# Three weight sums of a projection unit: made by GpSimd in the raw tiles, at product P6

## The chip, the cores and the metric

The kernel runs on one core of a Trainium2 chip. The metric is the device time of one execution in microseconds (us); of several timed runs the median stands. A core has five engines that run their own queues of instructions: TensorE (PE; its weight loads are listed apart, as PEld), VectorE (DVE), ScalarE (ACT), GpSimd (POOL) and SyncE (SP, which here only issues transfers). They wait for one another through semaphores.

## The reference

One layer of a hybrid trunk over 2048 positions of width 1024, all in 32-bit floating point. Cut to what matters here:

```
xn = rmsnorm(x, norm1_g)
z  = xn @ w_in                      # 1024 x 4608, this is the projection of the change
u_pool, zq, zf, zi, zo, zg = split(z)
gates  = sigmoid(zg + b_gate)
ya = pool_mixer(u_pool) @ w_pa
yb = hgrn2_mixer(zq, zf, zi, zo) @ w_pb      # gated linear recurrence, in chunks
x  = x + (gates[0] * ya + gates[1] * yb) @ w_o
x  = x + conv_glu_ffn(rmsnorm(x, norm2_g))
return rmsnorm(x, final_g)
```

## The kernel before, in words

**Products.** A product of two 32-bit matrices is made from three PE products of a reduced format (`fp32r`): each 128x512 weight tile is split into a high part, which ACT makes with a cast (L231, `ops`), and a low part, which DVE makes by subtracting the high part from the original (L232). PE multiplies both with a split activation (`mm`, L148 in the trace).

**Units.** The projection `z = xn @ w_in` is cut into fourteen *units* (the table `PROJ`: kinds `fq`, `g` and `u`). A unit is two 128-column blocks of outputs; its weights are four *quarters* q0, q1, q2, q3 of 128x512. A scheme of Strassen's kind makes the 2x2 block product with seven products instead of eight. Four of them need a sum of quarters as their weight: P6 takes s2 = q0+q2+q3, P5 takes s1 = q2+q3, P7 takes s3 = q0+q2, and P3 takes s4 = s2+q1; P1, P2 and P4 take q0, q1 and q3 as they are. The order of a unit's products is P1, P6, P5, P7, P2, P4, P3 (`ORDER`). Their results stand in three PSUM banks: X (P1, P2), Z (P6, P7, P4) and V (P5, P3). After P1 ACT copies bank X to `e1`; after P6 DVE makes `u2` = e1 - Z (L1196, `u` in the trace), and after P7 it makes `u3` from Z (L1200); P7 and P4 can only overwrite bank Z when that is done. The names in the trace are `fr`, `gr` and `ur` for units of kinds `fq`, `g` and `u`.

**Two passes.** The sequence is worked in two halves. In the first pass (from about 97 to 500 us) the quarters are loaded by SP (L197) into *raw* tiles, and the four sums of each unit are made by POOL, one add each (L444, function `comb`). Each sum is also stored to DRAM by SP (L341, `kw...`), and in the second pass (from about 1357 us) the sums are simply loaded from there.

**Buffers.** Raw tiles turn in a ring of eight (`N_RAW`), converted weights in one of six (`N_OPS`), and everything else that is 128x512 (sums, gates, intermediate results of the recurrence) takes one of 77 *slots* (`N_SLOTS`), in the order in which they are asked for. A tile is free for its next owner when all that read it, stores included, has ended.

**What sets the order.** The program is written as a stream of conversions that runs up to four weight tiles ahead of PE (`LOOKAHEAD`): `convert` calls the product's function `fn`, which may issue adds, and then the cast and the subtraction; `load_ahead` issues raw loads as soon as the ring has a tile whose last reader has been converted; `store_kept` issues the stores of the sums that `keep` has listed. Besides the units run tasks, stepped every six matmuls, for the heads of the recurrence: on PE `pl` (L1026, attention), `po` (L1125 and L1127), `pt` (L1144); on DVE `f` (L1096), `ss` (L1117), `ot` (L1138); on ACT `oh` (L1146), the gates `gt` (L1446); on POOL the copies `qm` (L1011), the products `q` (L1409) and the roots `ro` (L690); on SP the loads of `v` and `z` (L968) and of `mx` (L961). A scheduler then puts the instructions of each engine in the order in which its own estimate lets them run, so an edit in one place can change the order of an engine elsewhere. After the units come the products `pa` and `pb`, in which DVE makes `ya` (L1519) from the gates `gl` (L961).

Of the kernel before, what the change touches and what calls it, by code (L numbers as in the profile page):

```python
# [81 lines left out]
def tile_trunk(  # L82
# [26 lines left out]
    def slot(name, cols=TB, dt=F32):  # L109
        return slots.tile([P, cols], dt, tag="s", name=name, padded_shape=[P, 528])  # L110
# [221 lines left out]
    def keep(key, t, later=False):  # L332

        nm = "kw" + "".join(str(c) for c in np.ravel(key[1])) + f"{key[0]}{key[2]}"
        kept[key] = dram.tile([P, 512], F32, tag=nm, name=nm)
        keeping.append((kept[key], t, later))
# [12 lines left out]
    SUM_OF = {"P5": "s1", "P6": "s2", "P7": "s3", "P3": "s4"}  # L349
# [42 lines left out]
    def plan_unit(key, src, kind, i, order, b0):  # L392
        mv, mg = proj_tiles(kind, i)
        if b0:
            unit = sums_of_unit(src, mv, mg, lambda p: lambda: kept["in", (kind, i), SUM_OF[p]])
        else:
            unit = weights_of_unit(src[mv], src[mg], (kind, i))
        for p in order:
            fn, raws = unit[p]()
            stream.op(key, fn, raws)  # L400
# [19 lines left out]
    def quarters(src_v, src_g):  # L420
        return [s[:, c * 512 : (c + 1) * 512] for s in (src_v, src_g) for c in range(2)]
# [10 lines left out]

    def weights_of_unit(src_v, src_g, unit):
        src = quarters(src_v, src_g)
        raws, tmp = {}, {}

        def raw(i):
            if i not in raws:
                raws[i] = stream.raw(src[i])
            return raws[i]  # L440

        def comb(nm, key, x0, x1):
            t = slot(f"{nm}{key}")
            pool.tensor_tensor(t, x0, x1, ALU.add)  # L444
            tmp[key] = t
            keep(("in", unit, key), t)
            return t

        def plan(p):
            if p == "P5":  # L450
                return (lambda nm: tmp["s1"]), []
            rs = [raw(i) for i in {"P1": (0,), "P2": (1,), "P4": (3,), "P6": (0, 2, 3),
                                   "P7": (0, 2), "P3": (1,)}[p]]

            def fn(nm):
                t = [r.tile for r in rs]
                if p == "P6":
                    comb(nm, "s1", t[1], t[2])
                    return comb(nm, "s2", tmp["s1"], t[0])
                if p == "P7":  # L460
                    return comb(nm, "s3", t[1], t[0])
                if p == "P3":
                    return comb(nm, "s4", tmp["s2"], t[0])
                return t[0]

            return fn, rs

        return {p: (lambda p=p: plan(p)) for p in ORDER}

    def up_order():  # L470
# [1407 lines left out]
```

## Time and profile before

| | |
|---|---|
| median of 3 timed runs | 2531.32 us (2531.08 to 2533.26) |
| the profiled execution | 2530.39 us, its span 2528.7 us |
| PE busy | 2507.8 us, 99% of the span |
| weight loads of PE | 2053.8 us, 81% |
| DVE busy | 1963.1 us, 78% |
| ACT busy | 1195.1 us, 47% |
| POOL busy | 746.3 us, 30% |
| granted clock of PE | 0.999 |

The span runs from the first to the last instruction in the trace; the execution's own time is 1.7 us longer. All times within the trace are counted from the start of the span. In lists of instructions stand the start, the duration, the engine, the line, the operation, and in brackets how long the engine had been idle before and what ended that. In a list of waits stand the waiting instruction, what released it, the sum of the waits, their number and the longest. In a chain of work each row is released by the one above it. A table of stretches gives each stretch's bounds and length, then the busy time and the number of instructions of PE, PEld, DVE, ACT and POOL, the granted clock, the share of the transfer engines and their GB/s.

### The profile page before, as it was taken

The numbers are of one execution on the slowest core, as the hardware profiler recorded it, in microseconds if no ns is written. First come the engines' busy times: TensorE is split into PE (matmuls) and PEld (weight loads), VectorE is DVE, ScalarE is ACT, GpSimd is POOL, SyncE is SP. The second block draws the span as 40 slices with busy tenths as digits, with TensorE's granted clock in tenths as the row PEclk, the third lists the DMA queues.
The fourth block names the chain that finished last, engine by engine and source line by source line (L and its number), as shares of the span: only waits on it lengthen the run. The fifth ranks groups of instructions, "written<-read, shape, count | busy, mean of one in ns | idle before, by whom it ended". The sixth has DMA issues, their size and how long they took to land.

```text
span 2528.7 us, 35641 instructions
## 1 busy us (share of the span) xinstructions
PE 2507.8 (99%) x11508; PEld 2053.8 (81%) x11508; DVE 1963.1 (78%) x3476; ACT 1195.1 (47%) x2250; POOL 746.3 (30%) x1127
## 2 busy tenths in 40 slices
PE   9999999999999999999999999999999999999998
PEld 7888888788888888888888888888888888888887
DVE  7788878598898777885596778665979988778755
ACT  6534443334555454554554444542355554445534
POOL 4333453003354334451320202200033432325410
PEclk9999999999999999999999999999999999999999
DMA  8877777777898879997344343447443454447852
GB/s 272 271 184 231 203 203 231 221 230 244 200 259 231 229 230 240 265 364 244 123 150 150 109 134 109 138 148 233 140 155 118 151 153 135 153 133 245 321 166 97
DMA packets 252331, 493.75 MB, mean 195 GB/s; under 512 B 26544, under 2 KB 43056, under 8 KB 251824
## 3 DMA queue, kind: packets, MB, share of 16 engines
q1 hardware_dynamic: 184512, 313.60, 39.2%
q0 software_dynamic: 42656, 112.74, 17.5%
q10 hardware_dynamic: 24976, 65.13, 7.5%
q8 instruction: 91, 1.49, 0.2%
q14 instruction: 96, 0.79, 0.1%
HBM read 381.79 MB, written 187.17 MB: 225 GB/s over the span
## 4 chain that ended last, share of the span: by engine, by line
PE 92%; DVE 3%; DMA 1%; ACT 1%; issue 1%; POOL 0%; SPq 0%; ACTq 0%; DVEq 0%; POOLq 0%
PE dn_P L148 16%; PE up_Z L148 15%; PE up_V L148 10%; PE up_X L148 10%; PE wo_P L148 6%; PE gr_Z L148 4%; PE pb L148 4%; PE pa L148 3%; PE gr_X L148 3%; PE io_Z L148 3%; PE gr_V L148 3%; PE fr_Z L148 2%; PE io_V L148 2%; PE fr_X L148 2%; PE fr_V L148 1%; PE pl L1026 1%
## 5 line engine op out<-in xcount | busy, mean ns | idle before, releaser
L231 ACT CAST ops<-raw 128x512 fp32r<-128x512 f32 x744 | 459.6, 621 | 816.0 <-PE dn_P L148 179.5
L232 DVE TENSOR_TENSOR ops<-raw,ops 128x512 fp32r<-128x512 f32 x744 | 555.3, 750 | 216.7 <-ACT ops L231 209.8
L1614 DVE SCALAR_TENSOR_TENSOR e<-h,cols,e 128x512 f32<-128x512 f32 x176 | 143.3, 819 | 31.0 <-ACT e L1612 25.4
L1612 ACT ACTIVATE e<-h,cols 128x512 f32<-128x512 f32 x176 | 142.2, 814 | 25.1 <-DVE h L1159 18.3
L1617 DVE SCALAR_TENSOR_TENSOR e<-h,cols,e 128x512 f32<-128x512 f32 x176 | 133.9, 770 | 2.5
L961 POOL DMA_DIRECT2D g_P<-dg_P x154 | 84.0, 547 | 159.8 <-PE dn_P L148 111.3
L1269 POOL TENSOR_TENSOR gf_P<-e,e 128x512 f32<-128x512 f32 x44 | 61.2, 1392 | 149.4 <-DVE e L1623 95.9
L1269 POOL TENSOR_TENSOR gf_P<-gf_P,e 128x512 f32<-128x512 f32 x44 | 59.3, 1347 | 71.9 <-DVE e L1623 71.5
L1409 POOL TENSOR_TENSOR q<-q,qs 128x512 f32<-128x512 f32 x16 | 21.6, 1347 | 187.5 <-ACT qs L1408 180.3
L1607 POOL COPY h<-h 128x2 f32<-128x2 f32 x88 | 39.9, 466 | 117.7 <-DVE h L1158 113.6
L1621 ACT ACTIVATE e<-e 128x512 f32<-128x512 f32 x88 | 55.6, 632 | 38.3 <-DVE e L1617 38.0
L1446 ACT ACTIVATE gt<-gt,cols 128x512 f32<-128x512 f32 x48 | 34.8, 725 | 79.5 <-DVE gt L1159 47.1
L1609 POOL COPY hist<-h 128x2 f32<-128x2 f32 x88 | 35.5, 404 | 117.9 <-DVE h L1159 116.1
L1159 DVE TENSOR_TENSOR h<-up_u,up_V 128x512 f32<-128x512 f32 x88 | 60.1, 683 | 10.3 <-PE up_V L148 9.8
L1244 DVE TENSOR_TENSOR x<-x,wo_P 128x512 f32<-128x512 f32 x88 | 56.0, 681 | 12.1 <-PE wo_P L148 11.9
L1244 DVE TENSOR_TENSOR ac<-ac,dn_P 128x512 f32<-128x512 f32 x72 | 47.1, 681 | 16.7 <-PE dn_P L148 16.5
L1011 POOL COPY qm<-q 128x64 f32<-128x64 f32 x64 | 26.2, 437 | 96.9 <-DVE q L1043 18.2
L1637 POOL DMA_DIRECT2D dg_P<-gf_P x88 | 50.8, 577 | 8.1 <-POOL gf_P L1269 7.4
L1194 ACT COPY up_e<-up_X 128x512 f32<-128x512 f32 x44 | 25.8, 587 | 57.7 <-PE up_X L148 52.6
L1607 POOL COPY h<-hist 128x2 f32<-128x2 f32 x88 | 44.2, 510 | 27.4 <-DVE m_T42l L657 27.3
L1026 PE MATMUL pl<-qm,k 128*128 128x192 f32 x256 | 50.6, 326 | 1.0 <-DVE at L1037 0.9
L1026 PEld LDWEIGHTS pl<-qm,k 128*128 128x128 f32 x256 | 44.0, 189 | 6.2 <-POOL u L925 1.2
(1285 smaller groups left out, 8084.9 us busy)
## 6 DMA issues: line engine op xcount, KB each, us to landing
g_P<-dg_P POOLq DMA_DIRECT2D x154, 256.0 KB, 6.0
raw<-in_w_up_t SPq DMA_DIRECT2D x132, 256.0 KB, 3.3
raw<-in_w_in_t SPq DMA_DIRECT2D x98, 256.0 KB, 3.4
dg_P<-gf_P POOLq DMA_DIRECT2D x88, 256.0 KB, 3.9
dg_P<-e SPq DMA_DIRECT2D x66, 256.0 KB, 3.5
raw<-in_w_dn SPq DMA_DIRECT2D x66, 256.0 KB, 3.6
x<-in_x SPq DMA_DIRECT2D x64, 256.0 KB, 4.6
gd<-gt ACTq DMA_DIRECT2D x64, 256.0 KB, 3.2
```

The costliest lines, as they stand in the source:

```text
L148: count[1] = pe.matmul(*args, **kw)
L231: self.mark = act.copy(hi, v)
L232: low = self.low = dve.tensor_tensor(lo, v, f32(hi), ALU.subtract)
L961: eng.dma_start(t, d)
L1026: ins = pe.matmul(pa_[:, c * 192 : c * 192 + 192], ks[:, (i + c) * P : (i + c + 1) * P], mv[:, c].rearrange("p s x -> p (s x)"), start=Tru ...
L1159: return dve.tensor_tensor(dst, t, ps, ALU.add if how == "add" else ALU.subtract)
L1244: dve.tensor_tensor(t, t, ps[j], ALU.add if sg > 0 else ALU.subtract)
L1269: pin(eng.tensor_tensor(t, x0, x1, op))
L1607: pool.tensor_copy(h[:, 0:2], hist[:, mt] if hf == 0 else hs[s, 0][:, TB : TB + 2])
L1612: in_turn(act.activation(t, h[:, 2:], AF.Identity, bias=col(o_cb + mt), scale=col(o_cw + 4 * MF + mt)))
L1614: in_turn(second(dve.scalar_tensor_tensor(t, h[:, 1 : 1 + TB], col(o_cw + 2 * MF + mt), t, ALU.mult, ALU.add)))
L1617: dve.scalar_tensor_tensor(t, h[:, 0:TB], col(o_cw + mt), t, ALU.mult, ALU.add)
```

## The change

The sums are the same values up to rounding, made from other intermediate sums, at other places and into other tiles:

| sum | before | after |
|---|---|---|
| s1 = q2+q3 | at P6, into a slot | at P6, third, into the raw tile of q2 |
| s2 = q0+q2+q3 | at P6, s1 + q0, into a slot | at P6, second, s3 + q3, into a slot |
| s3 = q0+q2 | at P7, into a slot | at P6, first, into the raw tile of q0 |
| s4 = s2+q1 | at P3, into a slot | at P3, into the raw tile of q1 |

A sum is listed for its store when the product that uses it is converted (before: when it is made). The raw tiles of q0 and q2 now have their last use at P7 and P5, that of q1 at P3. One line of code less stands above, so after the change the lines of the trace are one lower (L443 for the adds).

```
-        def comb(nm, key, x0, x1):
-            t = slot(f"{nm}{key}")
+        def comb(key, t, x0, x1):
             pool.tensor_tensor(t, x0, x1, ALU.add)
-            tmp[key] = t
-            keep(("in", unit, key), t)
+            made[key] = t
             return t
 
         def plan(p):
-            if p == "P5":
-                return (lambda nm: tmp["s1"]), []
-            rs = [raw(i) for i in {"P1": (0,), "P2": (1,), "P4": (3,), "P6": (0, 2, 3),
-                                   "P7": (0, 2), "P3": (1,)}[p]]
+            rs = [raw(i) for i in {"P1": (0,), "P6": (0, 2, 3), "P5": (2,), "P7": (0,),
+                                   "P2": (1,), "P4": (3,), "P3": (1,)}[p]]
 
             def fn(nm):
-                t = [r.tile for r in rs]
                 if p == "P6":
-                    comb(nm, "s1", t[1], t[2])
-                    return comb(nm, "s2", tmp["s1"], t[0])
-                if p == "P7":
-                    return comb(nm, "s3", t[1], t[0])
+                    q0, q2, q3 = (r.tile for r in rs)
+                    comb("s3", q0, q0, q2)
+                    comb("s2", slot(f"{nm}s2"), q0, q3)
+                    comb("s1", q2, q2, q3)
                 if p == "P3":
-                    return comb(nm, "s4", tmp["s2"], t[0])
-                return t[0]
+                    comb("s4", rs[0].tile, made["s2"], rs[0].tile)
+                if p not in SUM_OF:
+                    return rs[0].tile
+                t = made[SUM_OF[p]]
+                keep(("in", unit, SUM_OF[p]), t)
+                return t
```

How this stands in the engines' queues is shown at three places, in the scheduled order. A row has the line, the operation, the tile written and the tiles read, with the numbers of the tiles.

The first is POOL in the third unit, whose quarters q0, q2, q3, q1 are raw45 to raw48. Before:

```order
L444 TENSOR_TENSOR w44s1_1609<-raw46_1310,raw47_1333 128x512
L444 TENSOR_TENSOR w44s2_1612<-w44s1_1609,raw45_1258 128x512
L1011 COPY qm0_0_4_0_1623<-q0_0_1409 128x2x8x4
L1011 COPY qm0_0_4_2_1629<-q0_0_1409 128x2x8x4
L1011 COPY qm1_0_4_0_1640<-q1_0_1364 128x2x8x4
L1011 COPY qm1_0_4_2_1646<-q1_0_1364 128x2x8x4
L304 DMA sw0s1_1287<-in_w_o 512x1x512
L444 TENSOR_TENSOR w46s3_1698<-raw46_1310,raw45_1258 128x512
```

And after:

```order
L443 TENSOR_TENSOR raw45_1256<-raw45_1256,raw46_1308 128x512
L443 TENSOR_TENSOR raw46_1308<-raw46_1308,raw47_1330 128x512
L443 TENSOR_TENSOR w44s2_1604<-raw45_1256,raw47_1330 128x512
L1010 COPY qm0_0_4_0_1616<-q0_0_1405 128x2x8x4
L1010 COPY qm0_0_4_2_1622<-q0_0_1405 128x2x8x4
L1010 COPY qm1_0_4_0_1633<-q1_0_1361 128x2x8x4
L1010 COPY qm1_0_4_2_1639<-q1_0_1361 128x2x8x4
L304 DMA sw0s1_1285<-in_w_o 512x1x512
```

All three adds now stand together ahead of the head's copies, the first of them writes over q0 (the scheduler has put s1 ahead of s2 in this unit), and no add follows the transfer of the output weights' sums (L304).

The second is SP at the end of the fourteen units. raw99 to raw101 are the first weights of `pa` and of the next product; `kwg7ins3` and `kwg7ins4` are the stores of the last unit's s3 and s4. Before:

```order
L341 DMA kwg7ins3_4597<-w123s3_4595 128x512
L197 DMA raw99_4660<-in_w_pa_t 128x512
L961 DMA mx0_0_4662<-md0_0_2119 128x512
L961 DMA mx0_1_4691<-md0_1_2303 128x512
L197 DMA raw100_4689<-in_w_pa_t 128x512
L341 DMA kwg7ins4_4685<-w126s4_4683 128x512
L197 DMA raw101_4725<-in_w_pb_t 128x512
L968 DMA z0_3_4703<-zd0_0_291 128x4x128
L961 DMA mx0_2_4727<-md0_2_3963 128x512
```

And after:

```order
L341 DMA kwg7ins4_4643<-raw92_4151 128x512
L197 DMA raw99_4619<-in_w_pa_t 128x512
L960 DMA mx0_0_4621<-md0_0_2106 128x512
L197 DMA raw100_4647<-in_w_pa_t 128x512
L960 DMA mx0_1_4649<-md0_1_2289 128x512
L197 DMA raw101_4683<-in_w_pb_t 128x512
L967 DMA z0_3_4661<-zd0_0_291 128x4x128
L960 DMA mx0_2_4685<-md0_2_3930 128x512
```

The store of s4 now reads a raw tile (raw92, the last unit's q1) and stands ahead of all of these, and raw100, which takes that same tile of the ring, stands ahead of the second `mx` load.

The third is DVE where the heads' last work meets the first conversions for `pa`. Before:

```order
L657 TENSOR_TENSOR mxs1_3l_4891<-mx1_3_4888,mxs1_3h_4890 128x512
L1519 TENSOR_TENSOR ya0_0_4924<-gl0_0_0_4894,pa0_0_4906 128x512
L232 TENSOR_TENSOR ops133_5014<-raw99_4660,ops133_5014 128x512
L232 TENSOR_TENSOR ops134_5053<-raw100_4689,ops134_5053 128x512
L1138 SCALAR_TENSOR_TENSOR ot1_3_4957<-po1_3_4859,ro1_3_4874,z1_3_4787 128x128 x4
L1519 TENSOR_TENSOR ya0_4_4962<-gl0_0_4_4898,pa0_4_4930 128x512
L1517 SCALAR_TENSOR_TENSOR ya1_0_4977<-gl1_0_0_4896,pa1_0_4964 128x512
```

And after:

```order
L656 TENSOR_TENSOR mxs1_3l_4849<-mx1_3_4846,mxs1_3h_4848 128x512
L1518 TENSOR_TENSOR ya0_0_4882<-gl0_0_0_4852,pa0_0_4864 128x512
L1137 SCALAR_TENSOR_TENSOR ot1_3_4915<-po1_3_4817,ro1_3_4832,z1_3_4745 128x128 x4
L1518 TENSOR_TENSOR ya0_4_4920<-gl0_0_4_4856,pa0_4_4888 128x512
L1516 SCALAR_TENSOR_TENSOR ya1_0_4935<-gl1_0_0_4854,pa1_0_4922 128x512
L232 TENSOR_TENSOR ops133_4972<-raw99_4619,ops133_4972 128x512
L232 TENSOR_TENSOR ops134_5011<-raw100_4647,ops134_5011 128x512
```

The subtractions for `ops133` and `ops134` stood ahead of the last head's `ot`, on which the transposition `pt` waits; now they stand behind it.

More of the change, by code (lines that the diff above doesn't have):

```diff
@@ L434, in weights_of_unit @@
         src = quarters(src_v, src_g)
-        raws, tmp = {}, {}
+        raws, made = {}, {}
         def raw(i):
```

## The prediction

> **What bounds the kernel now.** I read the page's busy times first, then busy times by stage, then what TensorE (PE) waited for, and last the chain of work behind each of those waits.
>
> ```profile
> span 2528.7 us, 35641 instructions
> PE 2507.8 (99%) x11508; PEld 2053.8 (81%) x11508; DVE 1963.1 (78%) x3476; ACT 1195.1 (47%) x2250; POOL 746.3 (30%) x1127
> ```
>
> PE is busy for all but 20.9 us of the span, so whatever GpSimd (POOL) does can only give back part of those 20.9 us, or add to them. The four sums of a unit are made only in the first of the two passes (in the second they are read back), so the two passes are a comparison in one trace: the same fourteen units with and without POOL's sums. The stretches below run from the first matmul of the first unit to the first `pa` matmul, and from there to the first `pb` matmul, for pass one and then pass two.
>
> ```profile
> 97.50:444.20 346.70, 341.00 (x1721) 283.84 (x1721) 282.33 (x652) 146.77 (x320) 137.80 (x149) 1.00 0.78 218
> 444.20:499.70 55.50, 53.66 (x250) 43.79 (x249) 27.05 (x49) 18.63 (x43) 3.63 (x5) 1.00 0.76 238
> 1357.20:1703.40 346.20, 346.20 (x1768) 290.93 (x1768) 252.37 (x651) 153.82 (x334) 56.56 (x86) 1.00 0.43 129
> 1703.40:1748.70 45.30, 45.30 (x204) 36.87 (x203) 21.36 (x39) 13.08 (x28) 1.20 (x2) 1.00 0.67 217
> ```
>
> After each length stand the busy times of PE, PE's weight load, VectorE (DVE), ScalarE (ACT) and POOL. Pass one takes 402.2 us where pass two takes 391.5: **10.7 us is all that everything belonging to pass one costs**, and no version of these sums can return more. PE idles there for 5.7 + 1.84 = 7.54 us. DVE is 30 us busier in the first stretch (282.33 against 252.37) for the same 650 instructions, while POOL has 81 us more, about 1.45 us for each of its 56 adds. The waits of PE from 97 to 500 us:
>
> ```profile
> PE gr_Z L148 <- DVE gr_u L1196: 2.7, 4, 1.0
> PE pt L1144 <- DVE ot L1138: 1.8, 1, 1.8
> PE ur_Z L148 <- DVE ur_u L1196: 1.8, 1, 1.8
> PE pl L1026 <- DVE at L1037: 0.9, 1, 0.9
> PE fr_Z L148 <- DVE fr_u L1196: 0.3, 1, 0.3
> ```
>
> PE never waits for a converted weight here. It waits for DVE: mostly for the subtraction that empties bank Z after P6, which must be done before P7 writes that bank. So the question is what makes DVE late, and there are three answers.
>
> First, POOL's adds hold DVE. This is the chain before the wait at 387.08 us, and POOL at the same time:
>
> ```profile
> 381.87 0.41 DVE f L1096
> ...
> 384.99 1.43 DVE f L1096
> 386.43 0.61 DVE gr_u L1196
> ...
> 387.08 3.06 PE gr_Z L148 x12
> ```
>
> ```profile
> 383.41 1.30 POOL L444 TENSOR_TENSOR w114s<-raw,raw 128x512 f32<-128x512 f32 x1 [0.63 <-DMA kwg5ins<-w109s]
> 384.79 1.35 POOL L444 TENSOR_TENSOR w114s<-w114s,raw 128x512 f32<-128x512 f32 x1
> ```
>
> The same product on `f` takes 0.41 us alone and 1.43 us while the second add runs (384.79 to 386.14); it cost this evacuation 1.0 us, and PE waited 0.95 us. The two adds are P6's of the *next* unit, which depend on nothing but their loads. The Trainium skill has this in "SBUF — State Buffer", section "SBUF: two separate sides": GpSimd and a DVE operation with two SBUF inputs lock a shared port pair, and the later one "fully blocks" for the whole instruction. This trace agrees (1.43 against 0.41 us). By that rule alone three adds in a row would hold such an operation for up to 3 x 1.35 = 4.05 us and eat the gain below wherever that meets an evacuation; in the rows above one DVE operation passes between the two adds, so the sum goes by the rows.
>
> Second, slots. A sum in a slot keeps it until its store has landed:
>
> ```profile
> 135.40 7.57 DMA gd<-gt
> ...
> 143.13 0.07 POOL w46s L444
> ```
>
> ```profile
> 281.59 10.27 DMA kwg3ins<-w84s
> 291.97 0.70 ACT oh L1146
> ```
>
> ```profile
>   ACT gt L1446: 11.7, 1
>   DVE ss L1117: 4.2, 1
> ```
>
> The first pair stands in the chain of `pl`'s 0.9 us: `w46s` (an s3) waits for a gate's store to free its slot, and the copies behind it on POOL wait too. The second stands in that of `ur_Z`'s 1.8 us: `oh` waits for the store of `w84s`, an s4. The last two lines are the largest waits of other engines for the stores of the sums (L341).
>
> Third, plain queue order on DVE, in the chain of `pt`:
>
> ```profile
> 465.08 0.68 DVE ops L232
> 465.77 0.27 DVE ot L1138
> 466.04 0.04 issue
> 466.08 0.33 PE pt L1144
> ```
>
> **The change part by part.**
>
> *The adds.* Fifty-six before and after, at the same size. An add that writes over one of its inputs is in the trace, POOL's product `q` (L1409):
>
> ```profile
> L1409 POOL TENSOR_TENSOR q<-q,qs 128x512 f32<-128x512 f32 x16 | 21.6, 1347 | 187.5 <-ACT qs L1408 180.3 <-issue 7.2
> ```
>
> 1.35 us against the 1.45 above: nothing lost, and POOL has room.
>
> *The new wait of s3, and with it of P6.* s3 overwrites q0, so it waits until ACT and DVE have converted q0 for P1; s2 and s1 follow. Behind it on POOL stand the `qm` copies, the `q` products and the roots `ro`; DVE and ACT wait for those. Price in the first unit, whose lead is short, and in the last:
>
> ```profile
> 91.04 1.28 DVE L232 TENSOR_TENSOR ops<-raw,ops 128x512 fp32r<-128x512 f32 x2
> ...
> 423.42 1.29 DVE L232 TENSOR_TENSOR ops<-w121s,ops 128x512 fp32r<-128x512 f32 x2 [1.01 <-ACT ops L231]
> ```
>
> ```profile
> 94.16 1.12 ACT L231 CAST ops<-w29s 128x512 fp32r<-128x512 f32 x2
> ```
>
> ```profile
> 100.34 0.39 PE L148 MATMUL fr_Z<-x_T20h,ops 128*128 128x512 f32 x1
> ...
> 430.41 0.48 PE L148 MATMUL gr_Z<-x_T20h,ops 128*128 128x512 f32 x1
> ```
>
> P1's conversion in the first unit ends at 92.32 (the second of the two). Two adds of 1.35, a cast of 0.62 and a subtraction of 0.68 make 95.7; PE needs P6 at 100.34, so 4.7 us of cover remain. P5 now waits for the third add, to 97.0, and is needed 2.8 us after P6. In the last unit P6 was ready near 424.1 and is needed at 430.4; 6.3 us. I cost this at nothing; if DVE's queue ran more than 4.7 us late, each further microsecond would be PE's.
>
> *P7 and the slots.* P7 no longer waits for an add at its own time. Three slot tiles of each unit go, 42 in all, so `w46s` and `w84s` cannot hold anything through a slot any more. s2 keeps its slot, so some slot waits stay.
>
> *The stores, now out of raw tiles.* A raw's next load must wait for its sum's store, on SyncE's (SP) one queue, with the head loads (`v`, `z`), the `mx` loads and later weights behind it. Landing times of the stores (L341) and of the raw loads, a raw load with the add that first reads it (last unit), and the start of `pa`:
>
> ```profile
> DMA to landing us min/median/max: 2.0/5.0/10.6
> ```
>
> ```profile
> DMA to landing us min/median/max: 2.4/4.4/10.2
> ```
>
> ```profile
> 373.89 1.21 SPq L197 DMA_DIRECT2D raw<-in_w_in_t  x2
> ...
> 431.17 0.80 SPq L961 DMA_DIRECT2D mx<-md  x2
> ...
> 437.92 0.33 SPq L197 DMA_DIRECT2D raw<-in_w_pb_t  x1
> ```
>
> ```profile
> 408.27 1.71 POOL L444 TENSOR_TENSOR w121s<-raw,raw 128x512 f32<-128x512 f32 x1 [2.39 <-DMA raw<-in_w_pa_t]
> ```
>
> ```profile
> 454.29 3.94 PE pa L148 x17
> ```
>
> The load is issued 34 us before its first reader; even a store of 10.6 us ahead of it leaves 13 us after the slowest landing. The thinnest place is the end: the second `mx` load stood at 431.6 and now stands behind a `pa` load whose buffer holds the last s4. At the latest that is where the next load stands today, 437.9; 10.2 us to land and 1.3 us to split give 449.4, and `pa` now starts after the last unit's products, at about 454.3. Cost nothing, cover 5 us.
>
> *The moved adds.* In the order of the changed kernel, P6's adds cannot run before the next unit's P1 conversion, so they leave the place shown at 383 to 386 us. The same adds of the next unit stand just ahead of four of the six waits for `u` (1.79, 0.95, 0.46 and 0.26 us): 3.46 us.
>
> *The end.* DVE's `ot` now stands ahead of the two conversions (order of DVE, above): up to 1.84 us of `pt`.
>
> **The sum.** Removable: 3.46 (adds away from the evacuation) + 0.91 (`pl`, slot) + 1.84 (`pt`) = 6.2 us. What is late next is DVE itself: all its work and all 56 adds stay, and the three adds of a unit land somewhere else in the same queue. Bounds: 0 and 6.2; I take the middle, **-3.1 us**. The profiled execution took 2530.39 us, so 2527.3; the median of the timed runs is 0.93 us higher, so **2528.2 us**.
>
> **The rivals.**
> *The waits only move* (or the sums were never in the way): the chains above all end on DVE, which speaks for it; the 10.7 us between the passes speaks against. 2531.3 us.
> *Three adds meet another evacuation; slower.* After P1's conversion the next evacuation of bank Z is that of P7, due before P4. A third add holds one more DVE operation, 1.0 us by the 1.43 against 0.41 above, so a unit that is hit waits 3.46 / 4 + 1.0 = 1.87 us. Four units hit make 7.5 us, which is 1.3 us slower in all; from seven of the fourteen on it is over 5 us: 7 x 1.87 - 6.2 = +6.9, **2538 us**. For it: ten more microseconds of adds come in threes. Against: the evacuation itself reads PSUM and took only 0.61 us with POOL at work around it, and PE has no wait before P4 today.
> *All of PE's idle time goes*: -7.54, **2523.8 us**. Against it: two of the six waits for `u` (1.24 us) have no add of the next unit before them.
>
> **How the numbers follow.** About 0.2% (5 us) is what a measurement of this kernel can tell from no change: below 2526.3 is faster, above 2536.4 slower. Forecast 0.60, of which 0.10 falls below 2526.3; waits that only move 0.15; three adds 0.18, of which 0.17 beyond 2536.4; all idle time gone 0.07, of which 0.06 faster. Faster 0.16, same 0.67, slower 0.17. The range reaches from 2523.8 to 2538.
>
> **What would show it.** Right: PE's waits for `u` and `pt` between 97 and 500 us fall from 7.5 to some 4 us; `oh` and `w..s` no longer wait for stores of sums; pass one's two stretches add to about 399 us; P6's adds start right after P1's conversion. Wrong: PE waits for converted weights (ACT or DVE `ops`), or for `u` before P4; `mx` late; the second pass differs from before at all.

## The result, and the profile after

The changed kernel takes **2521.95 us** (median of 6 runs, 2521.01 to 2522.33), the kernel before in the same runs 2531.94 (2531.08 to 2533.26). The ratio is 0.9959, with a 95% interval of 0.9947 to 0.9972: about 10 us faster, three times the forecast, and below the range.

First the page's busy times, then the same four stretches as before (first unit to first `pa`, to first `pb`, in both passes).

```profile
span 2520.5 us, 35649 instructions
PE 2506.8 (99%) x11508; PEld 2055.4 (82%) x11508; DVE 1943.3 (77%) x3476; ACT 1196.0 (47%) x2250; POOL 747.0 (30%) x1127
```

```profile
98.30:444.60 346.30, 346.30 (x1769) 291.19 (x1768) 270.74 (x661) 151.93 (x334) 140.80 (x152) 1.00 0.79 224
444.60:490.00 45.40, 45.40 (x203) 36.86 (x202) 21.08 (x38) 13.45 (x29) 2.98 (x3) 1.00 0.80 248
1348.55:1695.00 346.45, 346.45 (x1769) 291.15 (x1768) 252.27 (x651) 153.71 (x334) 56.73 (x86) 1.00 0.43 129
1695.00:1740.45 45.45, 45.45 (x203) 36.83 (x202) 21.44 (x39) 13.08 (x28) 1.20 (x2) 1.00 0.68 218
```

Pass one now takes 391.7 us, as long as pass two (391.9), against 402.3 before: 10.6 us (from the first matmul of the first unit to the first `pb` matmul), nearly the whole of the 10.7 that separated the passes. PE is busy in all of it; the list of PE's waits from 97 to 500 us, eight waits before, is empty. DVE is busy for 291.8 us in pass one, where it was 309.4, though the number and the size of the adds are the same. The span as a whole became only 8.2 us shorter (2520.5 against 2528.7): 0.7 us are lost ahead of pass one and 1.6 behind it, in the two executions that were traced, and I have not followed these.

Set matmul by matmul against the trace of before, pass one gains only at the eight places where PE waited:

| place (time in before, us) | PE idle there | gained there |
|---|---|---|
| `pl`, 152 and 154 | 0.09 + 0.91 | 1.49 |
| `gr_Z`, 206.7 | 0.92 | 1.18 |
| `gr_Z`, 283.1 | 0.32 | 0.50 |
| `ur_Z`, 311.6 | 1.79 | 2.05 |
| `fr_Z`, 362.5 | 0.26 | 1.25 |
| `gr_Z`, 387.1 | 0.95 | 1.21 |
| `gr_Z`, 413.7 | 0.46 | 0.82 |
| `pt`, 466.1 | 1.84 | 2.06 |
| sum | 7.54 | 10.56 |

So a wait costs more than its idle time. This is how the largest looks on PE:

```profile
308.80 0.39 PE L148 MATMUL ur_V<-x_T13h,ops 128*128 128x512 f32 x1
309.03 0.81 PE L1026 MATMUL pl<-qm,k 128*128 128x192 f32 x4
311.63 0.50 PE L148 MATMUL ur_Z<-x_T30h,ops 128*128 128x512 f32 x1 [1.79 <-DVE ur_u L1196]
311.96 0.39 PE L148 MATMUL ur_Z<-x_T30l,ops 128*128 128x512 f32 x1
312.19 0.39 PE L148 MATMUL ur_Z<-x_T30h,ops 128*128 128x512 f32 x1
```

Matmuls start 0.23 us apart and last 0.39 each, since they overlap. The idle time counts from the end of the last one, and after the wait the first lasts 0.50 and the second starts 0.33 behind it: some 0.26 us are lost that no row calls idle. At 362.5 a group of four transpositions also waited inside itself.

The same unit shows what changed. DVE and POOL before, then after, around `u2` (L1196, after L1195):

```profile
306.15 1.40 DVE L1017 TENSOR_TENSOR q<-qm,f 128x128 f32<-128x128 f32 x1
307.47 0.28 DVE L1037 COPY_PREDICATED at<-m,pl 128x128 f32<-128x128 uint8 x1
307.67 1.25 DVE L1017 TENSOR_TENSOR q<-qm,f 128x128 f32<-128x128 f32 x1
...
310.89 0.68 DVE L1196 TENSOR_TENSOR ur_u<-ur_e,ur_Z 128x512 f32<-128x512 f32 x1
```

```profile
305.91 1.49 POOL L444 TENSOR_TENSOR w93s<-raw,raw 128x512 f32<-128x512 f32 x1 [1.30 <-issue]
307.48 1.29 POOL L444 TENSOR_TENSOR w93s<-w93s,raw 128x512 f32<-128x512 f32 x1
```

```profile
304.28 0.68 DVE L1195 TENSOR_TENSOR ur_u<-ur_e,ur_Z 128x512 f32<-128x512 f32 x1
...
307.31 0.28 DVE L1016 TENSOR_TENSOR q<-qm,f 128x128 f32<-128x128 f32 x1
...
310.52 0.68 DVE L1199 TENSOR_TENSOR ur_u<-ur_Z,ur_e 128x512 f32<-128x512 f32 x1
311.12 0.29 DVE L1033 COPY_PREDICATED at<-m,pl 128x128 f32<-128x128 uint8 x1
311.32 0.68 DVE L1158 TENSOR_TENSOR u<-ur_u,ur_V 128x512 f32<-128x512 f32 x1
```

```profile
309.68 2.90 POOL L443 TENSOR_TENSOR raw<-raw,raw 128x512 f32<-128x512 f32 x2 [8.35 <-DVE ops L232]
312.53 1.30 POOL L443 TENSOR_TENSOR w93s<-raw,raw 128x512 f32<-128x512 f32 x1
```

Before, the next unit's two adds ran between the end of P6 and `u2`; two products of 0.28 us took 1.40 and 1.25, and PE waited 1.79. After, the three adds start when DVE has converted q0 (the releaser is `ops`, L232), 4.7 us behind the end of `u2`. There they lie beside the evacuation of P7 and the value after it, which both read PSUM and keep their 0.68 us.

For the experiments I worked out two numbers from each trace. The **delay** of `u2` runs from the end of P6's last matmul to its start; the **window time** is how much of POOL's adds falls into these fourteen delays. In the kernel before the delays add up to 43.9 us, six of them over 4 us, and the window time is 16.9 us; in the changed kernel it is 18.5 us, none over 3.2, and 0.0. A delay costs nothing as long as PE has other matmuls between P6 and P7: the twelve of P5 (2.8 us) and some of the heads. At the six waits of the kernel before, the delay less the wait is 3.4 to 4.2 us. This is a reserve in each unit: what stays within it is free.

### The profile page after: what moved, and what is told of

It reads as the page before. It is cut to its first block, busy times and chain, and to the rows that moved or that the text cites. A ratio compares the mean times of both kernels' runs of the same rounds, so it can differ in the third digit from the quotient of the medians.

```text
span 2520.5 us, 35649 instructions
## 1 busy us (share of the span) xinstructions
PE 2506.8 (99%) x11508; PEld 2055.4 (82%) x11508; DVE 1943.3 (77%) x3476; ACT 1196.0 (47%) x2250; POOL 747.0 (30%) x1127
## 3 DMA queue, kind: packets, MB, share of 16 engines
q8 instruction: 91, 1.49, 0.3%
## 4 chain that ended last, share of the span: by engine, by line
PE 98%; ACT 1%; POOL 0%; DVE 0%; DMA 0%; issue 0%; SPq 0%; POOLq 0%; DVEq 0%; ACTq 0%
PE dn_P L148 16%; PE up_Z L148 15%; PE up_X L148 10%; PE up_V L148 10%; PE wo_P L148 6%; PE gr_Z L148 5%; PE gr_V L148 4%; PE gr_X L148 4%; PE pa L148 4%; PE pb L148 4%; PE io_Z L148 3%; PE fr_Z L148 3%; PE fr_X L148 2%; PE io_V L148 2%; PE fr_V L148 2%; PE pl L1025 2%
## 5 line engine op out<-in xcount | busy, mean ns | idle before, releaser
L231 ACT CAST ops<-raw 128x512 fp32r<-128x512 f32 x786 | 485.4, 620 | 852.3 <-PE dn_P L148 180.2
L232 DVE TENSOR_TENSOR ops<-raw,ops 128x512 fp32r<-128x512 f32 x786 | 578.3, 738 | 226.1 <-ACT ops L231 219.8
L1606 POOL COPY h<-h 128x2 f32<-128x2 f32 x88 | 40.2, 468 | 117.5 <-DVE h L1157 110.6
L1608 POOL COPY hist<-h 128x2 f32<-128x2 f32 x88 | 35.5, 404 | 118.5 <-DVE h L1158 116.7
L443 POOL TENSOR_TENSOR raw<-raw,raw 128x512 f32<-128x512 f32 x28 | 38.9, 1390 | 102.0 <-DVE ops L232 101.0
L1010 POOL COPY qm<-q 128x64 f32<-128x64 f32 x64 | 27.1, 447 | 99.1 <-DVE q L1042 19.6
```

Source lines behind the costliest of these rows:

```text
L231: self.mark = act.copy(hi, v)
L232: low = self.low = dve.tensor_tensor(lo, v, f32(hi), ALU.subtract)
L1606: pool.tensor_copy(h[:, 0:2], hist[:, mt] if hf == 0 else hs[s, 0][:, TB : TB + 2])
```

## The experiments

All times are medians; "before" ran beside them at 2532.2 to 2533.6 us. "PE idle" is the sum of idle time in pass one.

| kernel | us | ratio to before (95%) | PE idle | delays of `u2`, sum / longest | window time |
|---|---|---|---|---|---|
| before | 2531.94 | 1 | 7.5 | 43.9 / 5.8 | 16.9 |
| changed | 2521.95 | 0.9959 (0.9947 to 0.9972) | 0.0 | 18.5 / 3.2 | 0.0 |
| order_slots | 2525.84 | 0.9975 (0.9965 to 0.9985) | 3.6 | 37.0 / 6.0 | 16.2 |
| tiles_old_times | 2538.95 | 1.0022 (1.0013 to 1.0031) | 10.5 | 42.7 / 10.0 | 12.5 |
| s3_only_tile | 2520.49 | 0.9952 (0.9940 to 0.9965) | 1.2 | 22.8 / 5.3 | 2.3 |
| no_adds | 2520.83 | 0.9954 (0.9941 to 0.9966) | 0.0 | 8.9 / 3.1 | none |
| wait_slots | 2524.56 | 0.9964 (0.9952 to 0.9976) | 3.3 | 27.6 / 5.3 | 1.9 |
| s4_only_tile | 2532.00 | 0.9998 (0.9989 to 1.0006) | 7.3 | 36.0 / 6.5 | 10.5 |
| before_wait | 2527.31 | 0.9979 (0.9970 to 0.9988) | 3.5 | 35.5 / 5.1 | 3.7 |
| before_late_store | 2533.01 | 1.0002 (0.9993 to 1.0011) | 8.0 | 40.2 / 6.0 | 12.9 |
| changed_again | 2521.33 | 0.9958 (0.9945 to 0.9970) | 0.0 | 17.8 / 3.2 | 0.0 |
| add_at_p7 | 2520.68 | 0.9955 (0.9942 to 0.9967) | 0.0 | 22.8 / 3.2 | 0.0 |
| before_halves | 2532.34 | 0.9999 (0.9990 to 1.0008) | 6.4 | 38.8 / 5.9 | 14.7 |
| s4_slot | 2520.68 | 0.9955 (0.9942 to 0.9969) | 0.1 | 22.1 / 4.1 | 1.5 |
| two_adds_p4 | 2520.22 | 0.9950 (0.9938 to 0.9962) | 0.7 | 31.6 / 4.0 | 4.1 |
| two_adds_behind | 2525.01 | 0.9966 (0.9954 to 0.9979) | 3.4 | 28.7 / 5.2 | 0.0 |
| before_wait_u | 2535.57 | 1.0011 (1.0002 to 1.0019) | 7.7 | 47.6 / 7.0 | 6.4 |
| two_adds_window | 2524.09 | 0.9968 (0.9956 to 0.9979) | 2.2 | 30.2 / 4.6 | 18.9 |
| two_adds_after_u | 2524.77 | 0.9972 (0.9962 to 0.9982) | 3.8 | 27.2 / 5.2 | 0.1 |

I began with two theories: **the slots** (a sum held its slot until its store had landed) and **the place** (where the adds run beside DVE).

**order_slots**: the new order and times, nothing overwritten.

```
-                    comb("s3", q0, q0, q2)
-                    comb("s2", slot(f"{nm}s2"), q0, q3)
-                    comb("s1", q2, q2, q3)
+                    s3 = comb("s3", slot(f"{nm}s3"), q0, q2)
+                    comb("s2", slot(f"{nm}s2"), s3, q3)
+                    comb("s1", slot(f"{nm}s1"), q2, q3)
...
+                    comb("s4", slot(f"{nm}s4"), made["s2"], rs[0].tile)
```

> The changed kernel with all four sums written into slots again: the same order of sums (s3, s2, s1 at P6, s4 at P3) and the same times of listing the stores, but no raw tile is overwritten, so no add waits for P1's conversion, and 42 slot tiles of 14 units are back. Theory of the slots (a sum's store held a slot, and whoever took the slot next made DVE late): the waits for u come back, about 2531 us. Theory of the place (it counts where the adds run beside DVE; s3 is no longer made at P7): most of the gain stays, 2522 to 2525 us; DVE's weight subtractions (L232) in pass one stay near 0.73 us each, against 0.83 before.

2525.84 us, a little above the range of the place: 6.5 us of gain without one freed slot. With no wait for P1's conversion the next unit's adds still reach the windows (16.2 us of them). PE's waits at 152 to 154 (`pl`), at 206, at 283 and for `pt` are gone all the same; they are 5.2 of the 10.6 us in the table above. So, by these traces, about half of the gain came with the new order and times of the sums, and not by emptying the windows.

**tiles_old_times**: before, with s3 over q2 at P7 and s4 over q1 at P3.

```
-                    return comb(nm, "s3", t[1], t[0])
+                    return comb(nm, "s3", t[1], t[0], t[1])
...
-                    return comb(nm, "s4", tmp["s2"], t[0])
+                    return comb(nm, "s4", tmp["s2"], t[0], t[0])
```

> The kernel before with its own order and times of the sums, but s3 written over q2 at P7 and s4 over q1 at P3; s1 and s2 keep slots. 28 of the 56 slot tiles go, the adds stay where they were. Theory of the slots: about two thirds of the ten microseconds come, 2525 us, as 28 of 42 slots are free. Theory of the place: the waits for u stay, 2530 to 2532 us, and L232 in pass one stays near 0.83 us.

2538.95 us, slower than before, though 28 slots are free; neither theory expected that. In the chain behind the longest wait (4.5 us, `pl`) stands an add of POOL. A store of a head's output, issued by ACT, with its time to landing; then POOL and DVE:

```profile
365.11 0.33 ACTq L956 DMA_DIRECT2D od<-oh  x1
```

```profile
DMA to landing us min/median/max: 7.6/7.6/7.6
```

```profile
372.83 1.28 POOL L444 TENSOR_TENSOR w107s<-raw,raw 128x512 f32<-128x512 f32 x1 [9.08 <-ACT qs L1408]
...
385.93 1.80 POOL L444 TENSOR_TENSOR w114s<-raw,raw 128x512 f32<-128x512 f32 x1
```

```profile
385.40 2.62 DVE L987 TENSOR_TENSOR q<-q,f 128x256 f32<-128x256 f32 x1
```

The store lands at 372.7 and the add `w107s` (s1, in a slot) starts at 372.83, having kept POOL idle for 9.08 us; the activation that the row names ended at 372.34. I read that as a slot wait of another kind: slots are taken in the order of asking, and with 28 askers gone this sum takes one that a head's output still holds. All that stands behind it on POOL is late, and the next adds meet the products of the next head: L987 takes 2.62 us. PE waits for `pl` only, and never for `u`. A good part of the loss is none of this: PE's granted clock was 0.5 for 17.0 us of pass one, which is told below.

**s3_only_tile**: the changed kernel with s3 alone in a raw tile.

```
-                    comb("s1", q2, q2, q3)
+                    comb("s1", slot(f"{nm}s1"), q2, q3)
...
-                    comb("s4", rs[0].tile, made["s2"], rs[0].tile)
+                    comb("s4", slot(f"{nm}s4"), made["s2"], rs[0].tile)
```

> The changed kernel with only s3 in a raw tile (over q0, so the wait for P1's conversion stays and the adds stand where they stand in the changed kernel); s1, s2 and s4 in slots. 14 of 42 slot tiles are freed. Theory of the slots: a third of the gain, about 2528.6 us. Theory of the place: all of it, 2522 us, with no wait of PE for u from 98 to 490 us.

2520.49 us: the whole gain with a third of the slots. Its one wait is told below.

**no_adds**: the four adds left out.

> The changed kernel without the four adds of each unit: a quarter stands in the place of each sum (q0 for s3 and s2, q2 for s1, q1 for s4), so GpSimd's 56 adds, the waits on them and 14 slot tiles are left out; the stores and the reading back stay. It says what the adds still cost where the changed kernel stands. Both theories: 2522 us within 1 us, since PE has no wait left in pass one; if the adds still hold something that the list of PE's waits does not show, up to 2 us less.

2520.83 us, pass one 391.5 us. The 56 adds cost the changed kernel nothing that can be measured, though without them DVE is busy for 275.7 us instead of 291.8.

**wait_slots**: order_slots, with s3's add waiting for P1's low half.

```
+        tc.add_manual_dep(ins.ins, stream.low.ins.name, mybir.DependencyInfo(
+            mybir.DependencyClass.Sync, mybir.DependencyReason.DATA), reason="after low")
...
-            pool.tensor_tensor(t, x0, x1, ALU.add)
+            ins = pool.tensor_tensor(t, x0, x1, ALU.add)
+            if key == "s3":
+                after_low(ins)
```

> The new order and times of the sums, all four in slots as in order_slots (2525.84 us), but the first add of a unit (s3) now waits for the low half of P1's conversion on DVE, as it does in the changed kernel because it overwrites q0. No slot is freed. Theory of the place: the wait itself makes the difference between order_slots and s3_only_tile, so about 2520.5 to 2522 us, and DVE's time in pass one falls from 353 to about 343 us (summed durations). Theory of the slots: the wait is nothing and the freed slots are what counts, so 2525.8 us or slower.

2524.56 us, between the two. The wait does what the place says: the window time falls from 16.2 to 1.9 us and DVE's summed durations from 353 to 342 us. But the 4 us to s3_only_tile remain, and the chain before the longest wait names a slot:

```profile
368.19 3.06 POOL w107s L448 x2
371.25 0.02 issue
371.27 9.10 DMA kwg5ins<-w107s
...
380.45 0.07 ACT k L980
...
381.44 1.21 PE pl L1072 x7
```

The head's tile `k` waits 9.1 us for a sum's store to leave the slot; PE waits 1.82 us, and behind that wait its granted clock was 0.5 for 3.4 us (below). In s3_only_tile the wait is gone. So the slots are a cause as well, once the adds are out of the way.

**s4_only_tile**: order_slots with s4 over q1.

> order_slots with s4 alone written over q1: 14 slot tiles are freed, as many as in s3_only_tile, without the wait for P1's conversion. Theory of the slots: the same gain as s3_only_tile, 2520.5 us. Theory of the place: no gain over order_slots, 2524 to 2527 us.

2532.00 us: as many slots freed as in s3_only_tile, and 6 us lost against order_slots. Here s4's add waits for P2's conversion and nothing holds back P6's adds (10.5 us in the windows). Two waits of PE stand out, 2.97 us for `pl` (159.2 us) and 2.42 for `u2` (391.7); ahead of both, the next unit's adds run beside DVE's products (`k`, L1046, takes 2.64 us, 0.55 alone, and L986 takes 1.54, 0.42 alone). Behind each of the two the granted clock was 0.5 for 3.4 us.

**before_wait**: before, with s1's add waiting for P1's low half (the same edit, `key == "s1"`).

> The kernel before with one wait more: P6's first add (s1) waits for the low half of P1's conversion; s3 stays at P7, all sums in slots, order and stores as before. Theory of the place, if the wait alone sets the place: 2524 to 2527 us, with two of the three adds out of the way. If it takes the third add away from P7 too: no more than 3 us of gain, 2529 to 2532 us. Theory of the slots: 2532 us or slower.

2527.31 us: one wait more makes the kernel before 5 us faster. The window time falls from 16.9 to 3.7 us, and of the six waits for `u` three (1.79, 0.95 and 0.46 us) are gone, and so is `pl`'s 0.91. What stays:

```profile
PE pt L1151 <- DVE ot L1145: 1.8, 1, 1.8
PE gr_Z L148 <- DVE gr_u L1203: 1.3, 2, 1.0
PE fr_Z L148 <- DVE fr_u L1203: 0.3, 1, 0.3
```

`pt` is plain queue order on DVE, and so, in the main, is the 1.0 us at 206: the heads' work stands ahead of `gr_u`, and the one add beside it (203.80 us, 1.30 us long) makes one product 0.17 us longer (`k`, 0.64 against 0.47). The queues of DVE there, before and after:

```profile
203.63 0.73 DVE L1073 COPY_PREDICATED at<-md,pl 128x256 f32<-128x256 uint8 x1
204.16 0.81 DVE L1086 COPY_PREDICATED at<-m,pl 128x256 f32<-128x256 uint8 x1
204.75 0.64 DVE L1094 TENSOR_TENSOR k<-k,f 128x256 f32<-128x256 f32 x1
...
205.98 0.67 DVE L1196 TENSOR_TENSOR gr_u<-gr_e,gr_Z 128x512 f32<-128x512 f32 x1
```

```profile
202.35 0.68 DVE L1195 TENSOR_TENSOR gr_u<-gr_e,gr_Z 128x512 f32<-128x512 f32 x1
202.95 0.72 DVE L1072 COPY_PREDICATED at<-md,pl 128x256 f32<-128x256 uint8 x1
```

The scheduler has put `gr_u` ahead of `at` in the changed kernel. wait_slots and s3_only_tile keep the old order there and the wait (1.23 us in both).

**before_late_store**: before, with a store listed when its sum is used.

> The kernel before with only the listing of the stores moved: a sum's store is listed when the product that uses it is converted, as in the changed kernel, instead of when the sum is made (this matters for s1 alone, by one product). Both theories: 2532 us within 2 us. If SyncE's queue, held by a store that waits for its add, is a cause, it would show here as a gain of more than 3 us.

2533.01 us: no effect. The time at which the stores are listed is not a cause.

The next four ran beside each other; the first is the changed kernel again.

> The changed kernel itself, unaltered, on the chip of the three kernels below, so that they can be set against it. Every theory: 2521 to 2523 us, and DVE's summed durations in pass one near 339 us.

2521.33 us.

**add_at_p7**: an add more in each unit, at P7.

```
+                if p == "P7":
+                    pool.tensor_tensor(slot(f"{nm}x"), made["s3"], made["s3"], ALU.add)
```

> The changed kernel with one add more in each unit, at P7, where s3 was made before: s3 + s3 into a slot that nobody reads. No conversion waits for it, so it can act only by holding DVE and by what stands behind it on GpSimd. Theory of the place: what hurt before was that DVE is held there; 14 adds of 1.35 us hold DVE for 5 to 10 us more (339 us becomes 344 to 349) and PE waits again, 2523.5 to 2526 us. Theory of the wait (what hurt before was that P7's conversion, and DVE's queue behind it, waited for the add of s3): no loss, within 1 us of the changed kernel.

2520.68 us. DVE is held as expected (summed durations 352 us instead of 340), and it costs nothing: the delays of `u2` grow from 18.5 to 22.8 us and none passes 3.2. So "holding DVE costs" is too simple, and the place fails here as I had put it.

**before_halves**: before, each add in two halves.

```
-            pool.tensor_tensor(t, x0, x1, ALU.add)
+            for c in range(0, 512, 256):
+                pool.tensor_tensor(t[:, c : c + 256], x0[:, c : c + 256],
+                                   x1[:, c : c + 256], ALU.add)
```

> The kernel before with each add cut in two halves of 256 columns: 112 adds of about 0.7 us instead of 56 of 1.45. The sums are made at the same places, in slots. Theory of the place, by which an add holds a DVE operation with two SBUF inputs until it ends: no operation is held for more than about 0.7 us, DVE's summed durations in pass one fall from 360 to some 345 to 350 us, and the time to 2527 to 2530 us. Theory of the slots: 2532 us or a little more.

2532.34 us, no gain; the window time hardly falls (14.7 us), nor do DVE's summed durations (359 us). But an add of half the columns took 0.93 us (mean of 112) and not the 0.7 expected, so there were 104 us of adds instead of 81. Smaller adds at the same places are no cure.

**s4_slot**: the changed kernel with s4 in a slot.

> The changed kernel with s4 in a slot and s3 and s1 in raw tiles: 28 of 42 slot tiles freed; s4 no longer waits for P2's conversion. As s3_only_tile (14 freed) was 2520.49 us and the changed kernel (42 freed) 2521.95, the theory of the place says the slots make nothing more: 2520 to 2522.5 us. Theory of the slots: slower than the changed kernel by 1 to 3 us.

2520.68 us: s4's tile adds nothing to those of s3 and s1.

Then I took the place in a narrower form: adds cost if they stand ahead of `u2` on their engines, not behind it.

**two_adds_p4** and **two_adds_behind**: 28 adds more, at P4's conversion or behind s1.

```
+                if p == "P4":
+                    for i in range(2):
+                        pool.tensor_tensor(slot(f"{nm}x{i}"), rs[0].tile, rs[0].tile, ALU.add)
```

```
                     comb("s1", q2, q2, q3)
+                    for i in range(2):
+                        pool.tensor_tensor(slot(f"{nm}x{i}"), q2, q3, ALU.add)
```

> The changed kernel with two adds more in each unit at P4's conversion (q3 + q3 into slots that nobody reads). They are then queued on GpSimd just where DVE works towards u2, the evacuation after P6, as the adds of the next unit's P6 stood before. 28 adds, about 38 us of GpSimd. Theory of the place in its narrow form (only what holds DVE ahead of u2 costs, and before the adds stood there): PE waits for u come back, 2523 to 2528 us. Theory that any hold costs by its length: the same loss as in two_adds_behind. Theory of the slots: no loss, up to 1 us.

> The changed kernel with the same 28 adds more, but queued behind s1 at P6, so that they run behind the wait for P1's conversion: five adds in a row. Theory of the place in its narrow form: little loss, 2521 to 2523 us, as these places lie behind u2. Theory that any hold costs by its length: the same loss as in two_adds_p4.

The opposite came: 2520.22 us with the adds ahead of `u2`, 2525.01 with them behind. At P4 they run just before P6 ends (27.1 us of adds within the 3 us ahead of the windows, 4.1 in them), and DVE has caught up by the time of `u2`:

```profile
301.91 2.21 POOL L459 TENSOR_TENSOR w90x<-raw 128x512 f32<-128x512 f32 x2
```

```profile
306.95 0.68 DVE L1198 TENSOR_TENSOR ur_u<-ur_e,ur_Z 128x512 f32<-128x512 f32 x1
```

P6 ends at 303.8 in this unit; the delay is 3.2 us, in the reserve. One unit is over it: PE waits 0.66 us for `u2` at 281.8 us.

In two_adds_behind PE waits 3.43 us in pass one. With five adds in a row behind P1's conversion it waits 0.89 us before P4 (214.0 us), where the adds hold a product (L1097, 1.35 us, 0.40 alone), and 0.56 for `pl`. But 1.40 us for the last unit's `u2` and 0.56 before its P4 are no holds: DVE had been idle, its queue standing behind conversions of `mx`, which had landed late. two_adds_after_u (below) has the same, 1.37 and 0.85 of its 3.78 us; this is its chain there:

```profile
423.19 8.24 DMA mx<-md
...
431.45 0.63 ACT mxs_0h L655
...
432.71 0.69 DVE gr_u L1195
```

In the changed kernel that load was issued at 420.99, and ACT's cast of it began at 425.67. What made it late I have not followed (two_adds_p4 takes as many slots more and has no such wait). So the loss of these two is not all the price of adds behind `u2`.

**before_wait_u**: before_wait, but waiting for the latest evacuation instead of P1's conversion.

> The kernel before with P6's first add waiting for the latest evacuation (u2 or u3) that stands ahead of it in the program, in the place of P1's conversion. Theory of the place: it is the adds ahead of u2 that cost, so this gives what before_wait gave (2527.3 us), 2526 to 2529 us. If the wait for P1's conversion works in another way (by spacing POOL's adds), 2530 us or more.

2535.57 us. The window time falls to 6.4 us, yet the time rises. Its longest wait (2.5 us, `pm`) is a slot again: the store of a sum (`w53s`, added at 166.5 us) takes 8.2 us to land, and `p` on DVE, which takes that slot next, waits for it until 177.6. Behind this wait too the clock was 0.5 for 3.4 us. Keeping the adds away from `u2` is not enough; what waits for them elsewhere must have time too.

**two_adds_window** and **two_adds_after_u**: the 28 adds in the windows, or just behind them.

```
             elif p == "P6":
+                if self.name[:3] in ("fr0", "gr0", "ur0"):
+                    for i in range(2):
+                        x = self.tmp(f"x{i}")
+                        ins = pool.tensor_tensor(x, t["e1"], t["e1"], ALU.add)
+                        if not i:
+                            tc.add_manual_dep(ins.ins, count[1].ins.name, ...)
```

> The changed kernel with two adds more in each unit (e1 + e1 into slots that nobody reads) that wait for the last matmul of P6, so that they start just where bank Z is ready and run while DVE works towards u2. In the kernel before 16.9 us of adds ran in these windows, in the changed kernel 0.0, in two_adds_p4 4.1. Theory of the window (an add costs only where it runs between P6's end and the start of u2): some 15 to 30 us of adds in the windows, waits of PE for u in at least five of the fourteen units, 2525 to 2532 us. In one unit, the one of the wait at 206 us of before, the queue of DVE has three more instructions ahead of u2, worth up to 1.2 us by itself. Against it: 2520 to 2522.5 us.

> The same two adds more in each unit, but u2 + e1, so that they wait for u2 itself and start just behind the window. Theory of the window: no add in the windows, next to no wait for u after P6, 2520.5 to 2523 us. If it is the length of the adds or GpSimd's own queue behind them that costs: as two_adds_window.

2524.09 and 2524.77 us: both lose 2 to 3 us against the changed kernel, so this pair doesn't separate them by time. The waits do: two_adds_window has 18.9 us of adds in the windows, and PE waits for `u2` twice (at least five waits were expected), 1.78 us in all. The larger, on POOL, DVE and PE:

```profile
277.65 2.19 POOL L1198 TENSOR_TENSOR gr_x<-gr_e 128x512 f32<-128x512 f32 x2 [1.28 <-PE gr_Z L148]
```

```profile
277.74 1.19 DVE L1095 TENSOR_TENSOR f<-f 128x128 f32<-128x128 f32 x1
278.85 1.54 DVE L232 TENSOR_TENSOR ops<-raw,ops 128x512 fp32r<-128x512 f32 x1
...
282.12 0.67 DVE L1203 TENSOR_TENSOR gr_u<-gr_e,gr_Z 128x512 f32<-128x512 f32 x1
```

```profile
282.85 0.50 PE L148 MATMUL gr_Z<-x_T30h,ops 128*128 128x512 f32 x1 [1.22 <-DVE gr_u L1203]
```

Two operations held by 0.8 us each, a late `u2`, a wait: the mechanism of before, put there by the edit. But window times of 16 to 19 us cost 4.7 us of waits for `u2` in before, 2.0 in order_slots and 1.8 here, so the window time alone doesn't give the price; how much of the reserve the rest of DVE's queue has used decides it too. two_adds_after_u waits in other places: `pl`, 1.1 us, a P4, 0.45, and the last unit, by the late `mx` (above).

**The granted clock** adds to some of these times. In pass one of six of the traces it was 0.5 for 3.4 us or a multiple of that, during waits of PE or at most 2 us behind them: 17.0 us in tiles_old_times, 6.8 in s4_only_tile and in before_halves, 3.4 in wait_slots, before_wait and before_wait_u. This is the one in before_wait, right behind the wait for `pt` (after the stretch's length the busy times; 0.50 is the clock):

```profile
461.70:465.10 3.40, 3.40 (x10) 2.66 (x10) 2.31 (x6) 0.00 (x0) 0.00 (x0) 0.50 1.10 272
```

Eight matmuls start 0.43 us apart there instead of 0.23, so these 3.4 us cost about 1.6 on top of the wait of 1.84. The same wait of 1.84 us in the kernel before had no such stretch behind it, and so it is with other waits of up to 2.0 us; which waits bring it on stays open. It explains what idle time leaves over: in before_wait PE idles 4.1 us less than in before, but pass one is only 3.4 us shorter. And of the 6 us that s4_only_tile loses against order_slots, 3.7 are more idle time and about 3 the clock.

**What is shown**, then: the adds themselves are nearly free where they stand in the changed kernel (no_adds, add_at_p7, two_adds_p4). Three of the waits for `u2` come from the next unit's adds between P6's end and `u2`: they go when a wait keeps the adds out (before_wait), and one of the kind comes when adds are put there (two_adds_window). Freed slots take away waits of another kind (wait_slots against s3_only_tile, before_wait_u). The waits at 206 and for `pt` went with DVE's order; that is read from its queues and not tested alone, and it is partly luck, as s3_only_tile keeps the wait at 206. **What stays open** is the exact share of each: they act on one reserve and don't add up. The wait for P1's conversion is worth 5 us on the kernel before, and only 1.3 us on order_slots, where a slot and the clock take some of it back.

## Why the prediction was wrong, by its own steps

- **The ceiling** was right: "10.7 us is all that everything belonging to pass one costs". 10.6 of it came.
- **The adds** at nothing: right. An add into its own input took 1.39 us on average:

```profile
L443 POOL TENSOR_TENSOR raw<-raw,raw 128x512 f32<-128x512 f32 x28 | 38.9, 1390 | 102.0 <-DVE ops L232 101.0
```

- **P6's new wait** at nothing: right. PE waits for no converted weight in the changed kernel. But it was entered as a risk with a cover of 4.7 us (its own terms, 92.32 + 2 x 1.35 + 0.62 + 0.68, make 96.3 and not 95.7, so 4.0), while before_wait shows that such a wait alone gains 5 us on the kernel before.
- **The stores from raw tiles** at nothing, and `mx`: right in the changed kernel. ACT waits for `mx` there, but no wait of PE comes of it. In two_adds_behind and two_adds_after_u it did come, 1.40 and 1.37 us, by a path that the prediction had not priced: not `pa`, but DVE's queue ahead of the last `u2`.
- **The slots**: half right. `pl`'s 0.91 us went, but it also went in order_slots, which frees none. A slot did cost 1.8 us elsewhere (wait_slots) and 2.5 in before_wait_u.
- **The moved adds**, 3.46 us: right in mechanism and too small. All six waits for `u` went, not four, and they gained 7.01 us. The two that I had left out (0.92 and 0.32 us, at 206 and 283.1) went too: at 206 by DVE's order, and at 283.1 the add of the unit's own s4, beside which a subtraction took 1.60 us (0.69 alone), stands there no longer. The 0.26 us at 362.5 I had counted wrongly: the next unit's add starts there only at 361.30 and holds nothing ahead of `u2`, and the wait stays in before_wait. DVE was late there beside the unit's own s4, too (`p`, 1.26 us, 0.17 alone).
- **The end**, up to 1.84 us: right, 2.06.
- **The sum failed**, twice; this is the step that was wrong. The prices were PE's idle times, 7.54 us, where the same waits cost 10.56; the difference of 3.1 us stood in the first table of the prediction, as 394.66 us of PE (341.00 + 53.66) in pass one against 391.5 in pass two, and I left it unexplained. And "Bounds: 0 and 6.2; I take the middle" halved the gain without a mechanism: "what is late next is DVE itself" was not so, since the delays of `u2` have a reserve that the moved adds no longer use up. Without the halving, and with the true price of a wait, the same list of terms gives 3.46 + 4 x 0.26 + 1.49 + 2.06 = 8.1 us.
- **The rivals**: "all of PE's idle time goes", with 0.07, is what happened, at a price 3 us too small. "The waits only move" fell. "Three adds meet another evacuation" fell for the changed kernel, since P7's evacuation reads PSUM and isn't held (0.68 us beside the adds); five adds in a row do make PE wait before P4 (two_adds_behind). The Trainium skill's rule in "SBUF — State Buffer", section "SBUF: two separate sides", speaks of a hold for one whole instruction; the prediction's 4 us for three adds in a row went beyond that. The trace agrees with the lock (1.40 and 1.25 us for products of 0.28), but the longest hold in pass one of the changed kernel, with its three adds in a row, is 1.1 us (`f`, 1.30 us against 0.16), and it is 1.1 in two_adds_behind with five; operations with one PSUM input keep their 0.68 us beside the adds.

## What to carry to other kernels

Price a stall by comparing the whole stage with a stage that lacks it, not by the idle time in front of the waiting instruction. Off-path work that contends with a busy engine costs by its place: look for the evacuation with the least reserve, and tie the work to an event that puts it elsewhere; then look at what it meets there. And where an edit changes a scheduler's order, ask what each wait was made of before taking a half of the sum.

## What the runs showed of the hardware that I had not expected

In the kernel before, most waits of PE cost about 0.26 us beyond their idle time, by the overlap of matmuls (0.23 us apart, 0.39 long) and a slower first one (0.50). In six other traces the granted clock fell to 0.5 for 3.4 us or more by a wait, and a wait of 1.84 us cost about 1.6 us more (before_wait). Fourteen or 28 adds more of GpSimd kept DVE busy for 11 to 15 us more in pass one (303.3 and 307.1 us against 291.8) and cost nothing in two places (2520.68 and 2520.22 us), and 2 to 4 us in three others, in two of these partly by a late `mx`.

```profile
98.11:490.18 392.07, 392.07 (x1969) 328.00 (x1968) 303.27 (x698) 165.37 (x362) 156.32 (x168) 1.00 0.80 227
```

```profile
98.63:491.29 392.66, 392.00 (x1970) 328.01 (x1968) 307.06 (x698) 165.27 (x362) 175.78 (x183) 1.00 0.80 226
```

These are pass one of add_at_p7 and of two_adds_p4, in one stretch each: DVE (third busy time) nearly as busy as before the change, and PE with 0.0 and 0.66 us of idle time.
